# Moving the chunk inverses' traffic in DRAM from SP's queue to ScalarE's and GpSimd's queues in a two-layer hybrid backbone

## Chip, cores and metric

The kernel runs on one core of one Trainium2 chip. The metric is the device time of one execution in microseconds (us). The kernel before has a median of 2059.9 us over three runs (2052.24, 2059.9 and 2060.2 us).

## What is computed

A diffusion backbone of two layers over 512 latent tokens and 256 context tokens of width 1024, all in fp32. Each layer has a mixing sub-layer and a squared-ReLU MLP, with RMSNorm, adaLN shift and scale ahead of each and an adaLN gate behind it. Layer 0 mixes by a bidirectional RWKV-7 recurrence (8 heads of 64) beside windowed attention, layer 1 by neighbourhood and global attention. The change is in the recurrence, whose state is updated token by token:

```python
def step(state, inp):
    r_t, w_t, k_t, v_t, kk_t, a_t = inp
    sa = jnp.einsum('bhvk,bhk->bhv', state, -kk_t)
    state = (state * w_t[:, :, None, :] + sa[..., None] * (kk_t * a_t)[:, :, None, :]
             + v_t[..., None] * k_t[:, :, None, :])
    return state, jnp.einsum('bhvk,bhk->bhv', state, r_t)
```

The adaLN vectors are products of the conditioning with w_ada, 6144 columns per layer.

## The kernel before

The recurrence is computed in chunks of 64 tokens, 12 chunks for the 768 tokens, for four pairs of heads (p = 0 to 3) and two directions d. Inside a chunk the update is a unit triangular system of 64 x 64. `prep(p, ...)` makes what the chunks of a pair need, in these stages:

- The front: loads of k and r from a DRAM scratch (849, 850), the heads' norm, the low-rank decays (865) and scans along the tokens (877, 879).
- The factors AR and BK on VectorE (903, 908), then the products of line 917 on TensorE and their masking into the tile XI (918).
- Per pair, four transfers write the two 32 x 32 diagonal blocks of each system from XI to the DRAM scratch nscr (925, 96 KB each in runs of 128 bytes), and one fetches them back as N (928, 384 KB), so that one system stands on each of 96 partitions.
- GpSimd sets X to the identity (930, 931) and makes two products (940, 947); VectorE makes BK's and AR's other halves (942, 945).
- The inverse: 31 steps of two VectorE instructions (954, 955). It ends with a transposed copy into N (958).
- X goes to the scratch xscr and N to tscr (959, 960); four transfers fetch the inverted blocks into XI (966) and two into xw (967).
- The merge: the off-diagonal block from products of 32 x 32 on TensorE (974, 982), in two halves q, with a ScalarE copy behind each product (xw behind 974, XI behind 982).

`chunks(p, ...)` uses XI: transposes (1023, 1029, 1040) of which one takes a value block vr that GpSimd (1038) and ScalarE copy, masked products AK (1052, 1053) and BT (1059, 1060), solving (1068, 1077), outputs (1089 to 1102), the passage from chunk to chunk (1015), and a step per chunk (1131, 1138). What prep makes in its second stage has two buffers, so that pair p+2 waits there for pair p's chunks.

The work is interleaved by generators: while pair p's chunks run, pair p+1's inverse, pair p-1's output and pair p+2's front are advanced, then pair p+2's second stage and pair p+1's merge. A third stream, `ada`, runs beside all of it as filler for TensorE: it loads w_ada in tiles w_raw of 512 KB through SP (341) into three buffers, multiplies each by the conditioning (353; one tile is four products in the program, eight in the profile), and finishes a group of four with a copy adar and a small product (362) and an addition into mod (364). The column products before that (430) stream their own weights through SP (238).

Within these bounds a scheduler of the language sets each engine's order, from its own estimates. Each engine runs its own instructions in order, and an engine that issues a transfer waits in its queue for what the transfer needs.

Of the kernel before, what the change touches and what calls it, by code (L numbers as in the profile page):

```python
# [174 lines left out]
def trunk(ctx: ExitStack, tc: tile.TileContext, xT, cT, vec_d, wada, we, wo_in, wout, wf1, wf2, lw2_d, la2_d, lg2_d,  # L175
          rpb_d, con_d, nm_d, rot_d, out):
    nc = tc.nc
    V, S, G, PE = nc.vector, nc.scalar, nc.gpsimd, nc.tensor
# [212 lines left out]
    nscr = dp.tile([4, 96, 32, 32], F32, name="nscr")  # L391
    xscr = dp.tile([4, 96, 32, 32], F32, name="xscr")
    tscr = dp.tile([4, 96, 32, 32], F32, name="tscr")
# [30 lines left out]
    def product(w, uh, ul, a, b, step=8):  # L424

        hi, lo = w
        ps = one()
        pairs = three(lambda k: hi[:, k, :], lambda k: lo[:, k, :], lambda k: uh[k][:, a:b], lambda k: ul[k][:, a:b], KT)
        for j, (x, y) in enumerate(pairs):
            PE.matmul(ps[:, 0:b - a], x, y, start=j == 0, stop=j == len(pairs) - 1)  # L430
            if j % step == step - 1 and j < len(pairs) - 1:
                yield
        return ps
# [409 lines left out]
    def prep(p, R, rt, iv, sts, res):  # L843
# [47 lines left out]
        xv = XI.rearrange("p c h t -> p (c h) t")  # L891
# [29 lines left out]
        for d in range(2):  # L921
            for b in range(2):
                o = d * 64 + b * 32
                i0 = d * 48 + b * 24
                nc.sync.dma_start(nscr[p, i0:i0 + 24].rearrange("i s t -> s i t"), xv[o:o + 32, :, 32 * b:32 * b + 32])

        N = iv.tile([128, 32, 32], F32, name="N")
        nc.sync.dma_start(N[0:96], nscr[p])
        X = iv.tile([128, 32, 32], F32, name="X")
        G.memset(X[0:96], 0.0)  # L930
        G.memset(X[0:96].rearrange("p a b -> p (a b)")[:, 0::33], 1.0)
# [18 lines left out]
        for s in range(31):  # L950
            a, b = s + 1, 31 - s
# [4 lines left out]
            if s % 2:  # L956
                yield QUIET if s > QS else None
        V.tensor_copy(N[0:96].rearrange("p s i -> p i s"), X[0:96])
        nc.sync.dma_start(xscr[p], X[0:96])
        nc.sync.dma_start(tscr[p], N[0:96])  # L960
        w1 = rt.tile([128, T], F32, name="xw")
        for d in range(2):
            for b in range(2):
                o = d * 64 + b * 32
                i0 = d * 48 + b * 24
# [311 lines left out]
    def front(p):  # L1277

        if p < 4:
            preps[p] = prep(p, R, rt, iv, sts, res)  # L1280
            yield from until(preps[p], FRONT)
# [188 lines left out]
    with ExitStack() as p2:  # L1470
# [17 lines left out]
        for p in range(4):  # L1488
# [42 lines left out]
            t = None  # L1531
# [215 lines left out]
    with ExitStack() as p3:  # L1747
# [13 lines left out]
        with pool("po", 1) as pp:  # L1761
            ws = [W.take() for _ in range(4)]
            po = [pp.tile([128, T], F32, name=f"po{m}") for m in range(6)]
            for ms, gs in ((range(4), GROUPS[:2]), ((4, 5), GROUPS[:2]), ((0, 1), GROUPS[2:])):
                for c, tok in gs:
                    while c == 1 and pend:
                        tick()
                    for m in ms:
                        if m == len(ws):
                            ws.append(W.take())  # L1770
                        p = product(ws[m], *u1, tok.start, tok.stop, 12)
# [119 lines left out]
```

## Time and profile before

| | |
|---|---|
| median of three runs | 2059.9 us |
| profiled execution | 2055.19 us |
| its span, and mean granted clock of TensorE | 2053.4 us, 0.971 |
| TensorE / VectorE / ScalarE / GpSimd busy | 94 / 55 / 40 / 6 % of the span |
| transfers issued by SP and ScalarE | 96544 and 15296 packets |

The span of the profiled execution is 1.8 us shorter than its own time, and that time is 4.7 us below the median. TensorE works at 94% of the span, and its idle time is what other engines and transfers can add. The column products run until some 346 us, the chunks of the four pairs from there until some 701 us, and the MLP and layer 1 after that. Rows of the profile give the start or the length in us, the engine (PE is TensorE, DVE VectorE, ACT ScalarE, POOL GpSimd, SP SyncE, and a q behind it the engine's queue), the line, and the tiles out<-in.

### The profile page before, as it was taken

The page shows a single profiled execution, that of the slowest core. Times are in us where ns is not written, and L with a number is a line of the kernel's source. Part 1 is how long each engine was busy: PE and PEld are TensorE (multiplying, and loading weights), DVE is VectorE, ACT ScalarE, POOL GpSimd, SP SyncE. Part 2 cuts the span into 40 slices and gives each one's busy share as a digit, 9 for nine tenths or more (in the row PEclk, how much of TensorE's full clock was granted, in tenths as well). Part 3 has the DMA queues.
Part 4 walks back from the last instruction along what each step waited for, and adds up shares of the span by engine and source line. Part 5 has one row for each costly group of instructions (what it writes and reads, how often), then busy time and mean ns, then how long its engine had stood idle before and what let it go on. Part 6 is the DMA issues. An engine that isn't in the chain of part 4 may idle for free.

```text
span 2053.4 us, 38620 instructions
## 1 busy us (share of the span) xinstructions
PE 1932.7 (94%) x16412; PEld 1633.5 (80%) x16412; DVE 1124.7 (55%) x1999; ACT 817.0 (40%) x1531; POOL 122.2 (6%) x149
## 2 busy tenths in 40 slices
PE   6999988988888899999999999899999899999997
PEld 3878767666666897888888889898888798888887
DVE  6576477547464377233433345856575575444445
ACT  3466442534335244311322122435686645222332
POOL 1000011011100000000000000001021000000000
PEclk9999989999999999999999999999999999999998
DMA  7422334666634233211221021342111334322221
GB/s 309 149 65 78 108 109 129 209 195 207 207 126 145 71 112 132 73 61 42 83 72 62 32 83 42 103 151 68 51 39 37 123 102 166 102 83 82 97 88 42
DMA packets 112013, 217.47 MB, mean 106 GB/s; under 512 B 38496, under 2 KB 63968, under 8 KB 111328
## 3 DMA queue, kind: packets, MB, share of 16 engines
q1 hardware_dynamic: 96544, 191.66, 28.6%
q10 hardware_dynamic: 15296, 23.33, 3.2%
q8 instruction: 129, 2.11, 0.4%
q14 instruction: 44, 0.36, 0.1%
HBM read 184.29 MB, written 28.05 MB: 103 GB/s over the span
## 4 chain that ended last, share of the span: by engine, by line
PE 63%; DVE 7%; ACT 3%; issue 3%; DMA 2%; POOL 1%; POOLq 0%; ACTq 0%; DVEq 0%; SPq 0%
PE x L1588 45%; PE x L430 5%; PE ax L530 2%; PE ax L511 2%; PE b L1015 1%; PE b L493 1%; PE ad L353 1%; PE b L1077 1%; PE b L494 1%; DMA w_raw<-in_wada_dram 1%; DVE X L955 1%; DVE nacc L288 1%; ACT Z L182 1%; DVE pr L954 1%; POOL r L264 0%
## 5 line engine op out<-in xcount | busy, mean ns | idle before, releaser
L182 ACT ACTIVATE w_hi<-w_raw 128x1024 fp32r<-128x1024 f32 x183 | 192.3, 1058 | 484.1 <-PE x L1588 369.1
L225 DVE TENSOR_TENSOR w_lo<-w_raw,w_hi 128x1024 fp32r<-128x1024 f32 x181 | 220.8, 1223 | 194.6 <-ACT w_hi L182 193.0
L1588 PE MATMUL x<-fl,w_hi 128*128 128x256 f32 (+1 forms) x864 | 290.9, 338 | 3.9 <-DVE fl L1675 3.9
L1588 PE MATMUL x<-uh,w_hi 128*128 128x512 f32 (+1 forms) x864 | 286.7, 337 | 3.0 <-ACT uh L182 3.0
L1588 PE MATMUL x<-fh,w_lo 128*128 128x256 f32 (+1 forms) x864 | 289.4, 336 | 0.0
L1588 PE MATMUL x<-ul,w_hi 128*128 128x512 f32 (+1 forms) x864 | 287.9, 336 | 0.0
L1588 PE MATMUL x<-uh,w_lo 128*128 128x512 f32 (+1 forms) x864 | 287.6, 336 | 0.0
L1588 PE MATMUL x<-fh,w_hi 128*128 128x256 f32 (+1 forms) x864 | 286.9, 337 | 0.0
L1602 DVE TENSOR_TENSOR oa<-x,oa 128x512 f32<-128x512 f32 (+1 forms) x184 | 103.1, 563 | 207.9 <-PE x L1588 207.0
L430 PE MATMUL x<-uh,w_hi 128*128 128x256 f32 (+1 forms) x560 | 190.2, 340 | 1.6 <-ACT po L182 1.3
L430 PE MATMUL x<-uh,w_lo 128*128 128x256 f32 (+1 forms) x560 | 189.1, 338 | 0.0
L430 PE MATMUL x<-ul,w_hi 128*128 128x256 f32 (+1 forms) x560 | 188.5, 337 | 0.0
L1588 PEld LDWEIGHTS x<-fl,w_hi 128*128 128x128 f32 x864 | 164.3, 190 | 22.0 <-DVE fl L1675 4.3
L1588 PEld LDWEIGHTS x<-uh,w_hi 128*128 128x128 f32 x864 | 161.8, 189 | 21.1 <-ACT uh L182 3.9
L1588 PEld LDWEIGHTS x<-fh,w_lo 128*128 128x128 f32 x864 | 164.1, 190 | 17.9
L1588 PEld LDWEIGHTS x<-fh,w_hi 128*128 128x128 f32 x864 | 162.1, 190 | 20.0 <-ACT fh L182 2.5
L1588 PEld LDWEIGHTS x<-ul,w_hi 128*128 128x128 f32 x864 | 162.8, 189 | 17.7
L1588 PEld LDWEIGHTS x<-uh,w_lo 128*128 128x128 f32 x864 | 162.8, 189 | 17.6
L430 PEld LDWEIGHTS x<-uh,w_hi 128*128 128x128 f32 x560 | 107.5, 192 | 12.5 <-issue 2.7
L430 PEld LDWEIGHTS x<-uh,w_lo 128*128 128x128 f32 x560 | 107.7, 192 | 9.4 <-issue 1.2
L430 PEld LDWEIGHTS x<-ul,w_hi 128*128 128x128 f32 x560 | 107.8, 192 | 9.2 <-issue 1.3
L1674 DVE TENSOR_TENSOR rl<-rl 128x512 f32<-128x512 f32 (+1 forms) x108 | 59.3, 550 | 77.7 <-ACT fh L182 77.5
(304 smaller groups left out, 3398.7 us busy)
## 6 DMA issues: line engine op xcount, KB each, us to landing
w_raw<-in_wf_dram SPq DMA_DIRECT2D x128, 512.0 KB
w_raw<-in_wada_dram SPq DMA_DIRECT2D x96, 512.0 KB
w_raw<-in_we_dram SPq DMA_DIRECT2D x21, 512.0 KB
w_raw<-in_wo_in_dram SPq DMA_DIRECT2D x18, 512.0 KB
w_raw<-in_wout_dram SPq DMA_DIRECT2D x16, 512.0 KB
hsc<-h ACTq DMA_DIRECT2D x8, 1024.0 KB
scr<-po ACTq DMA_DIRECT2D x21, 384.0 KB
h<-hsc SPq DMA_DIRECT2D x7, 1024.0 KB
```

Source lines behind the costliest of these rows:

```text
L182: return S.activation(o, i, f, **k)
L225: eng.tensor_tensor(o_lo, x, o_hi.bitcast(F32), op=ALU.subtract)
L288: V.tensor_reduce(acc, sq.rearrange("p k t -> p t k"), axis=AX.X, op=ALU.add)
L353: PE.matmul(ps[o:o + 32, 0:256], si[:, 2 * kp + k, :], w[:, k, j * 256:(j + 1) * 256], start=kp == 0, stop=kp == 3)
L430: PE.matmul(ps[:, 0:b - a], x, y, start=j == 0, stop=j == len(pairs) - 1)
L493: PE.matmul(ps[:, off:off + n], qs, kh, start=True, stop=False)
L494: PE.matmul(ps[:, off:off + n], qs, kl, start=False, stop=True)
L511: PE.transpose(pt[:, (kb - k0) * 128:(kb - k0 + 1) * 128], P[:, kb * 128:(kb + 1) * 128], ident)
L530: PE.matmul(po[h * 64:h * 64 + 64, 0:128], v(h, k), pts[h][:, k], start=k == 0, stop=k == n - 1)
L1588: PE.matmul(o, a, b, start=n == 0, stop=n == len(pairs) - 1)
L1602: tt(oa[:, m, tok], ps, oa[:, m, tok], op=ALU.add)
L1674: tt(r, r, r, op=ALU.mult)
```

## The change

The four writes of the blocks (925) are issued by ScalarE. The fetch of N (928) and the two writes of the result (959, 960) are issued by GpSimd (G). The fetches of the result (966, 967) and all weights stay with SP. Nothing of the data or the arithmetic is changed.

```diff
--- before.py
+++ after.py
@@ -922,10 +922,10 @@
             for b in range(2):
                 o = d * 64 + b * 32
                 i0 = d * 48 + b * 24
-                nc.sync.dma_start(nscr[p, i0:i0 + 24].rearrange("i s t -> s i t"), xv[o:o + 32, :, 32 * b:32 * b + 32])
+                nc.scalar.dma_start(nscr[p, i0:i0 + 24].rearrange("i s t -> s i t"), xv[o:o + 32, :, 32 * b:32 * b + 32])
 
         N = iv.tile([128, 32, 32], F32, name="N")
-        nc.sync.dma_start(N[0:96], nscr[p])
+        G.dma_start(N[0:96], nscr[p])
         X = iv.tile([128, 32, 32], F32, name="X")
         G.memset(X[0:96], 0.0)
         G.memset(X[0:96].rearrange("p a b -> p (a b)")[:, 0::33], 1.0)
@@ -956,8 +956,8 @@
             if s % 2:
                 yield QUIET if s > QS else None
         V.tensor_copy(N[0:96].rearrange("p s i -> p i s"), X[0:96])
-        nc.sync.dma_start(xscr[p], X[0:96])
-        nc.sync.dma_start(tscr[p], N[0:96])
+        G.dma_start(xscr[p], X[0:96])
+        G.dma_start(tscr[p], N[0:96])
         w1 = rt.tile([128, T], F32, name="xw")
         for d in range(2):
             for b in range(2):
```

The scheduler gives all engines another order between the last column products and the end of pair 3's inverse. Three places follow; the numbers behind a tile's name tell its instances apart.

VectorE around the inverse of pair 2, in pair 1's round (b_5034 is the AK product of block 0 of pair 1's chunks), before:

```order
L1053 TENSOR_TENSOR AK<-b_5034,con 128x384
L364 TENSOR_TENSOR mod<-ad,vec 128x8
L377 COPY sh<-mod 128x8 x2
L1060 TENSOR_TENSOR BT<-b_5048,con 128x12x64
L1199 TENSOR_TENSOR t<-b_5111,t 128x768
L942 TENSOR_TENSOR bk_4733<-kds,ei_4063 128x12x64
L948 SCALAR_TENSOR_TENSOR kds<-kds,vec,r 128x768
L364 TENSOR_TENSOR mod<-ad,vec 128x8
L954 TENSOR_TENSOR pr<-X,N 96x31
L955 TENSOR_TENSOR X<-X,pr 96x31
```

and now:

```order
L1201 TENSOR_TENSOR y<-y,r_5170 128x768
L364 TENSOR_TENSOR mod<-ad,vec 128x8
L954 TENSOR_TENSOR pr<-X,N 96x31
L955 TENSOR_TENSOR X<-X,pr 96x31
L954 TENSOR_TENSOR pr<-X,N 96x60
L955 TENSOR_TENSOR X<-X,pr 96x2x30
L954 TENSOR_TENSOR pr<-X,N 96x87
L955 TENSOR_TENSOR X<-X,pr 96x3x29
L954 TENSOR_TENSOR pr<-X,N 96x112
L1053 TENSOR_TENSOR AK<-b_5034,con 128x384
L955 TENSOR_TENSOR X<-X,pr 96x4x28
```

Seven instructions of the inverse stand ahead of AK, and the products 942 and 948 no longer stand between AK and its start. In SP's order, where pair 0's four writes were, there is now the load of r (850), with its wait for VectorE.

Pair 1's merge on ScalarE and on TensorE (b_4879 and b_4906 are the two halves of line 974, b_4937 and b_4964 those of 982). ScalarE before, with what each waits for (DMAHW are the counters of transfers that SP and ScalarE share):

```order
L182 ACTIVATE xw<-b_4879 32x384 [waits DMAHW5_49,DMAHW1_49,PE_49]
L182 ACTIVATE xw<-b_4879 32x384
L182 ACTIVATE xw<-b_4906 32x384 [waits PE_49]
L182 ACTIVATE adar<-ad 128x256 [waits PE_49]
L182 ACTIVATE xw<-b_4906 32x384
L182 ACTIVATE XI<-b_4937 32x12x32 [waits PE_49]
```

and now:

```order
L182 ACTIVATE adar<-ad 128x256 [waits PE_49]
L182 ACTIVATE xw<-b_4879 32x384 [waits PE_49]
L182 ACTIVATE xw<-b_4879 32x384
L925 DMA nscr<-XI 32x24x32 [waits DMAHW5_49,DVE_49]
L925 DMA nscr<-XI 32x24x32 [waits DMAHW0_49]
L925 DMA nscr<-XI 32x24x32 [waits DMAHW2_49]
L925 DMA nscr<-XI 32x24x32 [waits DMAHW5_49]
L182 ACTIVATE xw<-b_4906 32x384 [waits PE_49]
L182 ACTIVATE xw<-b_4906 32x384
```

The four writes of pair 2's blocks stand between the two halves' copies, and the fourth waits on the same counter as the first. TensorE in the same place before:

```order
L974 MATMUL b_4879<-xw,XI 32x32
L353 MATMUL ad<-w_raw,si 32x256 x4
L974 MATMUL b_4879<-xw,XI 32x32 x23
L974 MATMUL b_4906<-xw,XI 32x32 x24
L353 MATMUL ad<-w_raw,si 32x256 x4
L982 MATMUL b_4937<-XI,xw 32x32 x11
L362 MATMUL ad<-con,adar 128x4 x2
L982 MATMUL b_4937<-XI,xw 32x32 x13
L982 MATMUL b_4964<-XI,xw 32x32 x7
L353 MATMUL ad<-w_raw,si 32x256 x4
L982 MATMUL b_4964<-XI,xw 32x32 x17
```

and now:

```order
L974 MATMUL b_4879<-xw,XI 32x32 x22
L362 MATMUL ad<-con,adar 128x4 x2
L974 MATMUL b_4879<-xw,XI 32x32 x2
L974 MATMUL b_4906<-xw,XI 32x32 x17
L353 MATMUL ad<-w_raw,si 32x256 x4
L974 MATMUL b_4906<-xw,XI 32x32 x7
L982 MATMUL b_4937<-XI,xw 32x32 x3
L353 MATMUL ad<-w_raw,si 32x256 x4
L982 MATMUL b_4937<-XI,xw 32x32 x21
L353 MATMUL ad<-w_raw,si 32x256 x8
L982 MATMUL b_4964<-XI,xw 32x32 x24
L362 MATMUL ad<-con,adar 128x4 x2
```

Four tiles (x4, x4, x8) stand between the first products of 974's second half and 982's second half, where one stood before.

TensorE among the column products, some 270 us into the span, the difference:

```order
 L430 MATMUL x_2865<-ul_119,w_hi 128x256
 L430 MATMUL x_2865<-uh_111,w_lo 128x256
+L353 MATMUL ad<-w_raw,si 32x256 x16
+L362 MATMUL ad<-con,adar 128x4 x2
 L430 MATMUL x_2942<-uh_104,w_hi 128x512
 L430 MATMUL x_2942<-ul_112,w_hi 128x512
```

Four tiles in one go, with their finish, stand ahead of the columns x_2942; before, three of them stood behind those.

On GpSimd, N stands behind the products of line 947 in pair 0 and ahead of the copies vr of pair p-1's chunks in the later pairs; xscr and tscr stand ahead of the last of those copies.

## Rows read from the trace of the kernel before

**Rows 1.** Two lines of the profile page: the span, and the busy time of each engine with its share of the span.

```profile
span 2053.4 us, 38620 instructions
...
PE 1932.7 (94%) x16412; PEld 1633.5 (80%) x16412; DVE 1124.7 (55%) x1999; ACT 817.0 (40%) x1531; POOL 122.2 (6%) x149
```

**Rows 2.** Table by stretches (start:end in us, length, busy us of each engine with its instructions, granted clock of TensorE as a share of full speed, DMA share, GB/s): the end of the column products, then the four rounds of the chunked mixer.

```profile
269.00:346.00 77.00, 74.47 (x397) 60.33 (x395) 51.56 (x107) 22.55 (x31) 5.24 (x4) 0.89 0.41 123
...
360.00:380.00 20.00, 17.35 (x288) 13.89 (x287) 2.77 (x7) 9.95 (x21) 3.04 (x4) 0.74 0.45 117
380.00:420.00 40.00, 37.21 (x637) 24.19 (x635) 33.01 (x86) 18.40 (x31) 0.37 (x1) 1.00 0.79 263
...
448.00:475.00 27.00, 24.98 (x488) 16.61 (x482) 8.06 (x16) 12.61 (x26) 6.65 (x6) 0.87 0.77 225
475.00:520.00 45.00, 40.20 (x623) 27.75 (x615) 35.66 (x89) 19.36 (x31) 4.19 (x4) 0.92 0.59 200
...
548.00:578.00 30.00, 26.35 (x567) 18.54 (x568) 10.30 (x21) 12.71 (x26) 6.66 (x6) 0.89 0.60 177
578.00:620.00 42.00, 36.89 (x754) 28.47 (x754) 31.28 (x84) 12.46 (x27) 0.69 (x2) 1.00 0.47 137
```

**Rows 3.** What SP's queue waited for between 200 and 700 us: line, releaser, us in total, times, longest.

```profile
SPq L341 <- PE ad L353: 139.0, 51, 14.6
...
SPq L959 <- DVE X L955: 29.3, 3, 17.0
...
SPq L925 <- DVE XI L918: 25.5, 2, 24.3
...
SPq L341 <- DMA w_raw<-in_wada_dram: 22.2, 20, 3.3
```

**Rows 4.** SP's queue in time: pair 0's blocks, pair 1's result, pair 2's blocks, input, result and fetch, pair 3's blocks (start us, us, instruction, count).

```profile
269.31 3.03 SPq L925 DMA_DIRECT2D nscr<-XI  x4
...
414.49 0.34 SPq L959 DMA_DIRECT2D xscr<-X  x1
...
460.33 3.86 SPq L925 DMA_DIRECT2D nscr<-XI  x4
...
466.60 0.34 SPq L928 DMA_DIRECT2D N<-nscr  x1
...
510.06 0.34 SPq L959 DMA_DIRECT2D xscr<-X  x1
...
517.12 0.89 SPq L966 DMA_DIRECT2D XI<-xscr  x2
...
553.38 4.71 SPq L925 DMA_DIRECT2D nscr<-XI  x4
```

**Rows 5.** All issues of line 925 between 240 and 720 us: least/median/longest ns of one.

```profile
L925 SPq DMA_DIRECT2D nscr<-XI x16: 326/645/2067, 269.3 to 556.1; - x16
```

**Rows 6.** VectorE in time, pairs 2 and 3: the last mask of pair 2, the product block 0 of pair 1's chunk waits for, and the first step of the inverse of pairs 2 and 3.

```profile
448.47 0.69 DVE L918 TENSOR_TENSOR XI<-b,con 128x512 f32<-128x512 f32 x1 [0.50 <-PE b L917]
...
461.43 0.56 DVE L1053 TENSOR_TENSOR AK<-b,con 128x384 f32<-128x384 f32 x1 [7.78 <-PE b L1052]
...
474.66 0.18 DVE L954 TENSOR_TENSOR pr<-X,N 96x31 f32<-96x31 f32 x1
...
577.81 0.18 DVE L954 TENSOR_TENSOR pr<-X,N 96x31 f32<-96x31 f32 x1
```

**Rows 7.** Chain of waits that ended last, three pieces of it: start us, us, what.

```profile
441.54 5.57 DMA w_raw<-in_wada_dram
...
542.33 4.47 DMA w_raw<-in_wada_dram
...
583.99 5.76 DMA w_raw<-in_wada_dram
```

**Rows 8.** TensorE: all adaLN products between 345 and 701 us (count, busy us, mean ns, idle before them and its releasers); then pieces of the timeline in pair 1's merge, three of TensorE and two of ScalarE, and the first product of pair 2's merge.

```profile
L353 PE MATMUL ad<-w_raw,si 128*32 128x256 f32 x608 | 52.4, 414 | 7.1 <-DMA w_raw<-in_wada_dram 5.7 <-DVE mod L364 1.5
...
449.08 1.70 PE L974 MATMUL b<-xw,XI 32*32 32x32 f32 x94
450.71 0.64 PE L353 MATMUL ad<-w_raw,si 128*32 128x256 f32 x8
...
452.54 0.82 PE L982 MATMUL b<-XI,xw 32*32 32x32 f32 x40
...
450.06 1.48 ACT L182 ACTIVATE xw<-b 32x384 f32<-32x384 f32 x3 [1.16 <-PE b L974]
...
451.97 0.48 ACT L182 ACTIVATE xw<-b 32x384 f32<-32x384 f32 x1
...
549.93 0.75 PE L974 MATMUL b<-xw,XI 32*32 32x32 f32 x34
```

**Rows 9.** Beside one another: VectorE's product L908 alone and beside GpSimd's L940.

```profile
258.73 0.95 DVE L908 TENSOR_TENSOR bk<-t,ei 128x768 f32<-128x768 f32 x1
...
261.13 2.54 DVE L908 TENSOR_TENSOR bk<-t,ei 128x768 f32<-128x768 f32 x1
...
262.81 2.54 POOL L940 TENSOR_TENSOR t<-ic,k 128x768 f32<-128x768 f32 x1
```

**Rows 10.** GpSimd in time: two copies into a chunk's value block, one of pair 0's chunk and one (two instructions) of pair 1's, and the idle time before them with its releaser.

```profile
407.64 0.37 POOL L1038 COPY vr<-v 128x192 f32<-128x192 f32 x1 [29.30 <-PE b L1040]
...
460.67 0.46 POOL L1038 COPY vr<-v 128x64 f32<-128x64 f32 x2 [8.10 <-PE b L1040]
```

## Prediction

> **What bounds the kernel now.** I read the page first, then a table by stretches, then what SP's queue waited for, and last the timelines of single engines in the rounds that the change touches. The page says that TensorE is busy for 94% of the span and VectorE for 55% [rows 1]. So a transfer or an issue is worth only what it takes out of TensorE's idle time, and the reader should look for where that is. The table by stretches shows it [rows 2]. While the column products still run (269 to 346 us) TensorE idles 77.00 - 74.47 = 2.53 us in 77. In the rounds after that it idles more: 2.65 of 20, 2.79 of 40, 2.02 of 27, 4.80 of 45, 3.65 of 30, 5.11 of 42. All that this change can give lies there, and the three stretches in which the 31 steps of an inverse run on VectorE (380 to 420, 475 to 520, 578 to 620 us) hold 2.79 + 4.80 + 5.11 = 12.70 us of it.
>
> The waits of SP's queue come next, since the change is made there [rows 3]. SP stands 139.0 us for adaLN products of TensorE, because a weight buffer has to come free; that is SP running ahead, and costs nothing. It stands 29.3 us for the inverse's result (line 959) and 25.5 us for the masked blocks (line 925), and whatever is queued behind those waits is late. The price of that lateness is on TensorE's side: the 608 adaLN products between 345 and 701 us idled 5.7 us in all for a weight tile [rows 8]. The chain of waits holds landings of such tiles of 4.47 to 5.76 us [rows 7].
>
> **The change part by part.** *SP's queue freed.* It loses four issues per pair on line 925 (0.645 us median, 16 of them [rows 5]) and three more of 0.34 us [rows 4]. That is 4 x 0.645 + 3 x 0.34 = 3.6 us of SP per pair, on an engine that waits 139 us for TensorE, so it counts nothing. What can count is the idle time of 5.7 us for weight tiles. I take 0 and keep -5.7 as the bound: with three buffers, a tile's load starts when TensorE frees a buffer, and SP then has mostly nothing else before it. In pair 0 SP isn't even freed: where the blocks' issues stood (269.31 us [rows 4]) there is now the load of r, which itself waits for VectorE.
>
> *The inverse starts earlier in VectorE's order.* The new order puts the first seven of pair 2's instructions ahead of the AK product of pair 1's chunk, where before the whole inverse stood behind it. The trace says what that is worth: pair 2's last mask ended at 449.2 us, its blocks left SP only at 460.33, 11 us late, and N could be fetched at 466.60; the inverse began at 474.66, and pair 3's at 577.81 [rows 4, 6]. VectorE was busy for only 8.06 of the 27 us from 448 to 475 and 10.30 of the 30 from 548 to 578, and for 35.66 of the next 45 and 31.28 of 42 [rows 2]. Work moved from the full stretch into the empty one relieves the chunk's products that share VectorE with it. Bounds: 0, and the whole idle time of 12.70 us. I take half, -6.4 us, because part of that idle time is for ScalarE's copies and for weight tiles.
>
> *Four issues on ScalarE in the merge.* The blocks of pair p+1 now stand in ScalarE's queue among the copies xw and XI of pair p's merge, for three of the four pairs. Before, in pair 1's merge, three of the four copies went at 450.06 and the last at 451.97 us, and TensorE's second half of the merge followed closely [rows 8]. Now the four issues hold the copies behind them. Bounds of that hold: four issues at 0.645 us, 2.58 us, and the longest such group on SP, 4.71 us [rows 4, 5], plus a landing. The fourth issue waits on the same counter as the first (DMAHW5 in the order shown), and from the last block's issue (460.33 + 3.86 = 464.19) to the fetch of N (466.60) a landing takes at most 2.41 us [rows 4]; so 4.71 + 2.41 = 7.12 us at most. I take 4.71, pair 3's row, because it already has weight transfers beside it. TensorE has cover: four adaLN tiles of 0.64 us [rows 8] stand between the halves of the merge now, 2.56 us. Uncovered 4.71 - 2.56 = 2.15 us, in three merges +6.5 us; between 0 and 3 x 7.12 = 21.4 us.
>
> *A fourth adaLN tile among the column products.* TensorE now takes four tiles (16 products in the order) in one go. There are three buffers, so the fourth tile's load can be issued only when the first is used up. A landing takes 4.47 us, the two tiles between take 2 x 0.64: 4.47 - 1.28 = +3.2 us, between 0 (loaded in time by a longer lead) and 5.76 us, the longest landing shown [rows 7, 8].
>
> *Three issues on GpSimd.* The trace has no transfer issued from GpSimd. Its nearest row for GpSimd working beside VectorE is line 908: 0.95 us alone, 2.54 us beside a GpSimd product [rows 9]. If each of three transfers in the three later pairs slowed one VectorE instruction so, that is 9 x 1.59 = 14.3 us of VectorE time; only what falls into the inverse and isn't idle anyway reaches TensorE, and one instruction per pair, 3 x 1.59 = 4.8 us, is my upper bound. I take 0, as the fetch has slack: pair 2's result was fetched from 517.12 us on, and the merge that uses it began at 549.93 [rows 4, 8]. The page "GPSIMD Engine Reference" of the Trainium skill (section "1. Specifications") says that GpSimd's port to SBUF is shared with VectorE and that instructions with two SBUF inputs contend; line 908 agrees with it for arithmetic, 2.54 against 0.95 us, and whether writing descriptors does the same no row shows. By that rule all of the steps of an inverse, which have two SBUF inputs, would feel it, and the sum would be higher by up to the 4.8 us. The page "DMA: Bandwidth & Descriptors" (section "Specifications") speaks against the move too: it gives about 1 us to the first byte from GpSimd's queue and about 0.6 us from SP's or ScalarE's; by it each pair's chain of three would be some 1.2 us longer, an estimate from that page, and no row here shows it.
>
> **Sum.** 0 - 6.4 + 6.5 + 3.2 + 0 = +3.3 us. Against the profiled execution's own time, 2055.2 us (its span is 2053.4 [rows 1]), that makes 2058.5. The three timed runs have a median of 2059.9, 4.7 us higher, so on that scale **2063.2 us**. That is within 0.5% (10.3 us), which is about what a measurement of this kernel can tell from no change.
>
> **Rivals.** *A: the early inverse pays in full (faster).* All 12.70 us of idle time go, and the 5.7 us for weight tiles, while the ScalarE issues are covered and only the column stage's 3.2 us and one uncovered merge of 2.15 remain: -18.4 + 5.4 = -13.0, 2046.9 us. For it: VectorE stands nearly empty right before each inverse [rows 2]. Against: the merge can't start before the next round anyway, and the fetch had slack. Chance 0.18.
>
> *B: ScalarE's queue becomes the wait in each merge (slower).* The copies xw and XI feed the second half of the merge, and everything in the next chunk stands behind it on TensorE. If the cover of adaLN tiles fails, because its own fourth tile is late for the reason given above, each merge pays 4.71 us: 14.1 + 3.2, and nothing from the inverse, as what is gained there is lost at the next merge: +17.3, 2077.2 us. It decides when the copy behind the last block issue starts more than 2.56 us after the copy before the first one. For it: four issues in a row with waits on the counters between them. Against: in pairs 2 and 3 the blocks are ready close to the merge's start. Chance 0.22.
>
> *C: GpSimd's queue holds the chunk's copies.* GpSimd now waits for the end of the inverse to store xscr, and the copies vr of line 1038 are queued behind. In pair 0's chunk such a copy ran at 407.64 us and the store was possible only at 414.49 [rows 4, 10]; likewise pair 1's copies at 460.67 stood free and now follow N, which waits for the blocks to land. If the inverse isn't earlier, the copy is 6.9 us late, and the products of that block with it: +3.3 + 6.9 = +10.2, 2070.1 us. The earlier inverse speaks against it. Chance 0.10.
>
> *D: the change doesn't do what it says.* SP, freed of these waits, stands at the next one (r behind VectorE, the fetch behind xscr), all weights arrive as before and ScalarE's issues are hidden: 2059.9 us. Chance 0.05.
>
> **How the numbers follow.** My forecast has 0.45. A and the forecast's lower tail give 0.20 for faster; B, a part of C and the upper tail 0.28 for slower; the rest, 0.52, is within 0.5%. The range reaches from A's 2046 to somewhat beyond B, 2082, since B's hold has an upper end of 7.12 us a merge; the bounds of the other costs lie inside it.
>
> **What would show it.** Right: in pair 1's merge a gap of about 4.7 us between two xw copies, filled by the four issues, and TensorE idle for some 2 us there; pair 2's blocks leaving at about 451 instead of 460.33; its inverse starting near 465 instead of 474.66; a wait for a weight tile of about 3 us before 285 us; SP's waits for L918 and L955 gone from its list; less TensorE idle time in the three inverse stretches, by half. Wrong: the stretches after an inverse no shorter although it began 10 us earlier (the merge wasn't waiting for it); copies of line 1038 that wait for GpSimd's own queue (C); or steps of the inverse visibly longer beside GpSimd's issues.

## The result and the profile after

The changed kernel takes 2080.6 us (median of four runs, 2072.8 to 2082.3) against 2056.6 for the kernel before (four runs, 2052.2 to 2060.2): a ratio of 1.011, interval 1.0073 to 1.0147, so some 24 us slower. The fourth run has moved the median of the kernel before from 2059.9 to 2056.6 us. The forecast was 2063.2 us, 3.3 us over its base and within 0.5%; the measured time lies inside the stated range, near its upper end, and on the side that had a chance of 0.28.

The page of the changed kernel, answering to [rows 1]:

```profile
span 2080.3 us, 38638 instructions
...
PE 1947.6 (94%) x16412; PEld 1642.9 (79%) x16412; DVE 1125.4 (54%) x1999; ACT 816.9 (39%) x1531; POOL 130.8 (6%) x161
```

The span is 26.9 us longer and TensorE is still busy for 94% of it. So the loss is not simply idle time: 14.9 us of it are busy time, for the same 16412 products. Where it arises is seen best from the end of one pair's last mask (918) to the next one's, as every round has nearly the same work there (some adaLN tiles and a part of line 974 lie on another side of a border, so that rounds 1 and 2 compare best by their sum). First the kernel before (stretch, length, busy us of the engines from TensorE on, granted clock, DMA share, GB/s): the column products up to pair 1's mask, the rounds up to the masks of pairs 2 and 3, up to pair 3's merge, and up to the MLP:

```profile
269.30:357.60 88.30, 80.78 (x552) 64.44 (x552) 62.86 (x121) 24.64 (x37) 9.93 (x7) 0.86 0.44 133
357.60:449.20 91.60, 80.86 (x1569) 58.36 (x1563) 54.52 (x126) 38.87 (x73) 6.68 (x9) 0.94 0.65 200
449.20:551.00 101.80, 90.95 (x1656) 64.08 (x1654) 58.90 (x130) 38.76 (x74) 13.01 (x12) 0.92 0.63 202
551.00:622.30 71.30, 62.59 (x1276) 46.81 (x1268) 39.25 (x100) 24.64 (x53) 7.35 (x8) 0.95 0.52 152
622.30:691.40 69.10, 57.98 (x1268) 47.31 (x1263) 33.31 (x44) 34.84 (x60) 4.87 (x5) 0.93 0.31 103
```

and the changed kernel, with the same borders:

```profile
271.60:367.90 96.30, 83.51 (x544) 66.37 (x546) 62.15 (x123) 24.14 (x37) 12.13 (x10) 0.84 0.43 130
367.90:472.10 104.20, 87.04 (x1650) 61.98 (x1641) 55.58 (x126) 40.01 (x75) 8.93 (x12) 0.87 0.62 195
472.10:578.40 106.30, 95.95 (x1575) 66.07 (x1572) 58.84 (x128) 38.13 (x73) 15.33 (x15) 0.84 0.59 181
578.40:649.50 71.10, 63.06 (x1270) 47.68 (x1270) 40.19 (x98) 24.12 (x52) 9.72 (x11) 0.88 0.46 134
649.50:721.30 71.80, 60.24 (x1267) 49.94 (x1263) 33.01 (x44) 34.63 (x60) 3.98 (x5) 0.88 0.30 99
```

The five stretches grow by 8.0, 12.6, 4.5, -0.2 and 2.7 us, together 27.6 (449.7 against 422.1), rounds 1 and 2 by 17.1 (210.5 against 193.4). TensorE's busy time in them goes from 373.2 to 389.8 us (+16.6), its idle time from 48.9 to 59.9 (+11.0). The granted clock falls in each, from 0.86-0.95 to 0.84-0.88. A reader should stop at that column: products at the lower of TensorE's two levels, 1.2 and 2.4 GHz, count as busy, and a table of busy shares alone would hide them.

Which products they are, the table of groups says. All 640 adaLN products from 262 to 740 us before (count | busy us, mean ns | idle just before them, and its releasers), answering to the first row of [rows 8]:

```profile
L353 PE MATMUL ad<-w_raw,si 128*32 128x256 f32 x640 | 54.5, 412 | 7.1 <-DMA w_raw<-in_wada_dram 5.7 <-DVE mod L364 1.5
```

and after:

```profile
L353 PE MATMUL ad<-w_raw,si 128*32 128x256 f32 x640 | 67.5, 457 | 18.5 <-DMA w_raw<-in_wada_dram 14.7 <-DVE mod L364 3.7
```

13.0 us more busy and 11.4 us more idle time in front of them: a sum of 24.4 us, against the 26.9 that the span is longer, stands at this one line, the filler. It waits 14.7 us for weight tiles instead of 5.7. That is where the time shows, and not yet what causes it (e14 below).

SP's queue, answering to [rows 3] (line, releaser, us in total, times, longest):

```profile
SPq L966 <- DMA xscr<-X: 29.1, 4, 17.6
...
SPq L850 <- DVE kds L948: 21.1, 1, 21.1
```

The waits for 918 and 955 are gone. SP now waits 29.1 us for xscr to land (9.5 before), in place of the 29.3 for the inverse's end, and 21.1 us for VectorE's product 948, ahead of r. So SP is not much freer: these waits take 50.2 us instead of 64.3 (with the 25.5 of 918). What changed is the order of what it sends.

**The column products.** SP's load of k and TensorE's norm of it (405) before:

```profile
272.50 0.45 SPq L849 DMA_DIRECT2D k<-scr  x1
...
282.66 1.50 PE L405 MATMUL x<-con,t 128*128 128x2 f32 x12 [0.17 <-ACT t L182]
```

and now, SP in pair 0's place, then TensorE:

```profile
278.56 8.93 SPq L341 DMA_DIRECT2D w_raw<-in_wada_dram  x4
287.60 0.37 SPq L849 DMA_DIRECT2D k<-scr  x1
...
286.03 1.08 PE L353 MATMUL ad<-w_raw,si 128*32 128x256 f32 x8 [6.66 <-DMA w_raw<-in_wada_dram]
...
294.61 1.40 PE L405 MATMUL x<-con,t 128*128 128x2 f32 x12
```

The load of k, which before left SP right behind pair 0's blocks, stands behind four weight tiles and leaves at 287.60. The fourth adaLN tile on TensorE waits 6.66 us for its weights, and the norm of k follows at 294.61.

**Pair 0's merge.** ScalarE, then TensorE:

```profile
367.94 0.37 ACTq L925 DMA_DIRECT2D nscr<-XI  x1
369.90 0.84 ACT L182 ACTIVATE gl<-gl 128x768 f32<-128x768 f32 x1 [9.52 <-DVE go L380]
369.92 7.03 ACTq L925 DMA_DIRECT2D nscr<-XI  x3
377.06 0.38 ACT L182 ACTIVATE adar<-ad 128x256 f32<-128x256 f32 x1 [6.32 <-DMA nscr<-XI]
...
368.69 1.71 PE L974 MATMUL b<-xw,XI 32*32 32x32 f32 x96
373.66 0.64 PE L353 MATMUL ad<-w_raw,si 128*32 128x256 f32 x8 [3.26 <-DMA w_raw<-in_wada_dram]
377.49 1.01 PE L362 MATMUL ad<-con,adar 128*128 128x4 f32 x4 [3.20 <-ACT adar L182]
378.84 2.79 PE L353 MATMUL ad<-w_raw,si 128*32 128x256 f32 x24 [0.33 <-DVE mod L364]
381.55 2.23 PE L982 MATMUL b<-XI,xw 32*32 32x32 f32 x74
```

Behind the first issue stands gl, and behind it three issues that take 7.03 us; only then come adar and the copies xw. TensorE ends 974 at 370.4, waits 3.26 us for a weight tile and 3.20 for adar, works through three more tiles at 0.93 us each, and begins 982 at 381.55: 11.2 us between. Before, 982 followed 974 after 0.8:

```profile
359.83 0.24 PE L982 MATMUL b<-XI,xw 32*32 32x32 f32 x2 [0.79 <-ACT xw L182]
```

The chain of waits shows what became of the blocks:

```profile
367.94 8.68 DMA nscr<-XI
...
376.65 5.03 DMA nscr<-XI
...
382.20 6.95 DMA N<-nscr
```

The first block needs 8.68 us to land, the fourth, which waits on the first one's counter, 5.03 more, N 6.95. Before, all four had landed at most 6.1 us after the first issue (nscr issued at 357.63, N at 363.71).

**Pair 2**, answering to [rows 6] and to the forecast's marks (last mask and first step of the inverse on VectorE, the first two issues on ScalarE):

```profile
471.37 0.69 DVE L918 TENSOR_TENSOR XI<-b,con 128x512 f32<-128x512 f32 x1 [0.24 <-PE b L917]
...
489.17 0.19 DVE L954 TENSOR_TENSOR pr<-X,N 96x31 f32<-96x31 f32 x1 [4.46 <-DMA N<-nscr]
...
472.96 0.89 ACTq L925 DMA_DIRECT2D nscr<-XI  x2
```

The first issue follows the mask within 0.9 us instead of 11, and the inverse starts 17.1 us after it instead of 25.5. That part came as forecast, and bought nothing (e7 below).

### The profile page after: what moved, and what is told of

The parts are those of the page before. It is cut to its first block, busy times and chain, and to the rows that moved or that the text cites. A ratio compares the mean times of both kernels' runs of the same rounds, so it can differ in the third digit from the quotient of the medians.

```text
span 2080.3 us, 38638 instructions
## 1 busy us (share of the span) xinstructions
PE 1947.6 (94%) x16412; PEld 1642.9 (79%) x16412; DVE 1125.4 (54%) x1999; ACT 816.9 (39%) x1531; POOL 130.8 (6%) x161
## 4 chain that ended last, share of the span: by engine, by line
PE 76%; DVE 9%; issue 5%; DMA 5%; ACT 4%; POOL 1%; SPq 0%; POOLq 0%; ACTq 0%; DVEq 0%
PE x L1588 45%; PE x L430 11%; PE ax L530 3%; PE ax L511 2%; PE b L493 2%; DMA nscr<-XI 1%; PE ad L353 1%; PE b L494 1%; DMA w_raw<-in_wada_dram 1%; PE b L1015 1%; PE b L1077 1%; DMA N<-nscr 1%; PE b L865 1%; POOL r L264 1%; DVE pr L954 1%
```

## Experiments

All ratios are against the kernel before, on the same chip. The change itself has 1.011 (1.0073 to 1.0147) and 24.0 us.

| kernel | ratio, interval | us over before |
|---|---|---|
| e1: only the blocks on ScalarE | 1.0121 (1.0094 to 1.0147) | 26.3 |
| e2: only N, xscr, tscr on GpSimd | 1.0023 (1.0004 to 1.0041) | 5.4 |
| e4: only xscr, tscr on GpSimd | 0.9996 (0.998 to 1.0013) | -0.6 |
| e5: the change, N left to SP | 1.0066 (1.0043 to 1.0089) | 15.3 |
| e7: the change, AK ahead of the inverse | 1.0135 (1.0105 to 1.0166) | 26.7 |
| e12: the change, merges first | 1.018 (1.0146 to 1.0213) | 38.7 |
| e12b: before, merges first | 0.9996 (0.9983 to 1.0009) | -1.8 |
| e11: two of four writes on ScalarE | 1.0041 (1.0027 to 1.0056) | 7.4 |
| e14: the change, fourth tile behind the columns | 1.0128 (1.0108 to 1.0148) | 28.3 |
| e15: the change, merge's copies on VectorE | 1.0166 (1.0136 to 1.0196) | 35.9 |
| e10: the change, blocks on GpSimd too | 1.0063 (1.0045 to 1.0081) | 12.8 |
| e16: the change, three weight tiles used over and over | 0.9918 (0.9898 to 0.9937) | -15.2 |

### Which part: e1, e2, e4, e5

```diff
e1:  nc.scalar.dma_start(nscr...)   N, xscr, tscr: nc.sync
e2:  nc.sync.dma_start(nscr...)     N, xscr, tscr: G
e4:  nc.sync.dma_start(nscr..., N)  xscr, tscr: G
e5:  nc.scalar.dma_start(nscr...)   N: nc.sync   xscr, tscr: G
```

> Only the four writes of the blocks (925) go to ScalarE; N, xscr and tscr stay with SP. Theory A (ScalarE's issues and the order that they bring cost the time: four adaLN tiles in one go among the column products, 6.7 us of wait in the changed kernel, and the copies xw of pair 0's merge held behind the issues, some 11 us): most of the loss stays, 14 to 20 us over the kernel before. Theory B (the transfers that GpSimd issues are slow, N needs 6.7 to 7.8 us to land, and the inverse waits 26.8 us for it): within 5 us of the kernel before. Under both the inverse waits less for N than 26.8 us.

> Only N, xscr and tscr go to GpSimd; the four writes of the blocks stay with SP, and VectorE's order is nearly that of before, with no step of an inverse ahead of the AK product of block 0. Theory A: within 5 us of the kernel before, since an inverse that starts late anyway doesn't wait for N. Theory B: 12 to 24 us slower, as N lands some 3 to 4 us later in each of the four pairs and xscr, tscr as well.

> Only the result (xscr, tscr) goes to GpSimd; the rest stays with SP. Theory A: within 5 us of the kernel before, perhaps some us faster, since SP no longer stands 29.3 us for the end of the inverses and the fetch has 18 us and more of slack in pairs 0 to 2. Theory B: 3 to 8 us slower, by later landings ahead of pair 3's merge, which has no slack.

> The change with N left to SP: blocks from ScalarE, result from GpSimd. The order is that of the changed kernel, with the inverse ahead of AK. Theory A: near the first of these four kernels; against the changed kernel it gains only what N lands earlier in three rounds, 3 x 3 = 9 us at most, so 10 to 20 us over the kernel before. Theory B: N was the cost, so within 5 us of the kernel before.

The blocks on ScalarE alone cost as much as the whole change (26.3 us, more than the 14 to 20 expected). The result on GpSimd costs nothing, N some 5 us. Theory B fell. In e1 and e5, with the blocks on ScalarE, the scheduler's order is nearly that of the change (four tiles among the columns, steps of the inverse ahead of AK); in e2 and e4 it is nearly that of before. TensorE's wait for weight tiles in e1 is almost that of the change:

```profile
PE ad L353 <- DMA w_raw<-in_wada_dram: 13.9, 8, 4.8
```

e5 is 11 us better than e1, though it only adds the result on GpSimd, and 9 us better than the change, whose interval overlaps with its own; the first was not expected, and its cause stays open.

### ScalarE's hold or VectorE's wait: e7, e12, e12b, e11

```diff
e7   in prep, around the first L954:
+            with tc.issue_after(res["ak"].ins) if not s and "ak" in res else nullcontext():
     (and the round's generators start one step later, so that AK exists)
e12  the change, e12b the kernel before:
-        for t in until(preps[1], READY): ...
         for t in preps[0]: ...
+        for t in until(preps[1], READY): ...
     (and the same swap in rest())
e11
-  nc.scalar.dma_start(nscr...)
+  (nc.scalar if d else nc.sync).dma_start(nscr...)
```

> The change, and the first step of each inverse of pairs 1 to 3 may only stand behind the AK product of block 0 of the round's chunks on VectorE; ScalarE's issues stay inside the merges. Theory A1 (ScalarE's issues hold the merge's copies; by the profile of the changed kernel the merge of pair 0 is 10.8 us longer, the column products 6 to 9 us, and the rounds after it together only some 5.5 us): the loss stays above 14 us over the kernel before, at most 6 us better than the change. Theory A2 (VectorE's wait for N ahead of AK, 10.4 + 4.5 + 7.4 us in pairs 1 to 3, is the loss): within 8 us of the kernel before.

> The change, with the merge of each pair put ahead of the next pair's second stage in the program, so that the copies xw and XI stand ahead of the four issues on ScalarE; AK then also stands ahead of the inverse. Four adaLN tiles stay in one go among the column products. A1: pair 0's merge takes some 5 us instead of 17, and what is left is the column products' 7 us and N's late landing: 5 to 11 us over the kernel before. A2 expects the same total, but with the merge's length unchanged and the gain in the rounds; the first run beside this one tells the two apart. A third theory (A3: the adaLN tiles alone, six more us of waiting for weights, at any place): still 14 us and more over the kernel before.

> The kernel before, with the merge ahead of the next pair's second stage: the control for the run before this one, since that order may cost or gain by itself. A1 and A2 expect within 6 us of the kernel before; if the order itself is worth 6 us or more, the gain of the run before this one is not ScalarE's queue.

> The change, with the two writes of the blocks of direction 0 left to SP and two on ScalarE: the column products have the order of before again (three adaLN tiles). A1: two issues still stand among the copies of pair 0's merge behind the load of gl, so that merge is 5 to 10 us longer than before, and the column products lose nothing: 6 to 14 us over the kernel before. If the hold grows with the number of issues alone, half: about 5 us in that merge.

e7 took VectorE's wait for N nearly away. In the change:

```profile
DVE pr L954 <- DMA N<-nscr: 26.8, 4, 10.4
```

and in e7, where 954 has become line 955:

```profile
DVE pr L955 <- DMA N<-nscr: 5.2, 2, 3.8
```

The time stayed (26.7 us over). So the inverse ahead of AK is not the loss, A2 fell, and taking most of the 26.8 us of VectorE's waiting away gained nothing. e12 has xw and XI ahead of the issues and is the slowest of all, 38.7 us over; the order alone costs nothing (e12b). The hold only moved to the next copy that TensorE needs:

```profile
ACT adar L182 <- DMA nscr<-XI: 13.8, 2, 8.9
```

So my A1, too, had the wrong place: it isn't the merge's copies alone. e11 has no four tiles in one go, and TensorE's wait for weights is that of before; it costs 7.4 us, as A1 expected. So those 7.4 us are not TensorE's wait for weight tiles, and their cause isn't shown:

```profile
PE ad L353 <- DMA w_raw<-in_wada_dram: 5.5, 6, 1.6
```

### The tiles, the copies, the queue: e14, e15, e10

```diff
e14  in ada, around the products of the first group's fourth tile:
+                with tc.issue_after(lastcol[0].ins) if hold and (l, q, kp) == (*which[0], 3) else nullcontext():
e15  xw, XI and adar:
-            act(...)
+            V.tensor_copy(...)
e10
-  nc.scalar.dma_start(nscr...)
+  G.dma_start(nscr...)
```

> The change, with the fourth adaLN tile's products allowed on TensorE only behind the last column product; the merges' order on ScalarE stays. Theory C (four tiles in one go cost the column stage 8 us, of which 6.7 us are the wait for the fourth tile): the column stage back to 88 to 90 us from 96.3, and the whole 14 to 20 us over the kernel before instead of 24. If the tile was only a place where time was lost that something else loses next (the same weights are waited for later): still 22 us and more.

> The change, with the merge's copies xw and XI and the copy adar of the adaLN rows done by VectorE, so that nothing that TensorE waits for in a merge stands behind the four issues on ScalarE. Four tiles stay in the column stage. Theory A1 (ScalarE's queue, held by the issues and their counters, is what costs the rounds): round 1 (mask to mask) back from 104 to 92 to 96 us, and the whole 8 to 14 us over the kernel before, nearly all in the column stage. Theory A4 (the blocks land in 5 to 9 us instead of 3 beside the weights that SP now sends, and TensorE idles for that): round 1 still above 100 us, the whole 18 us and more over.

> The change, with the four writes of the blocks on GpSimd as well: SP is as free as in the change, ScalarE issues nothing of it. A1: within 8 us of the kernel before, less than the change by 16 us or more. A4: still 15 us and more over the kernel before, as the blocks land beside the same weights, and GpSimd's transfers land late (6.7 to 7.8 us).

e14 removed the wait for the fourth tile, and gained nothing. Its SP, ScalarE and TensorE show why:

```profile
276.63 1.28 SPq L341 DMA_DIRECT2D w_raw<-in_wada_dram  x3
278.01 1.15 SPq L852 DMA_DIRECT2D k<-scr  x1
...
288.47 0.93 ACT L182 ACTIVATE t<-k,vec 128x768 f32<-128x768 f32 x1 [11.01 <-DMA k<-scr]
...
289.46 2.72 PE L406 MATMUL x<-con,t 128*128 128x2 f32 x12 [9.56 <-ACT t L182]
```

k is issued behind three weight tiles at 278.01 and ScalarE's first use of it starts at 288.47; TensorE then stands 9.56 us at line 405. The tile's wait had only covered that of k. From pair 0's last mask to the norm of k (405) it is 13.4 us before, 23.0 in the change, 19.8 in e14 and 10.0 in e10, and the column stage lasts 88.3, 96.3, 92.9 and 81.8 us: the later k, the longer the stage (e10 also has less adaLN work there, 2.1 us in place of 4.6 before and 7.4 in the change). Rounds 1 and 2 take 211.3 us in e14, as in the change.

TensorE's wait for weight tiles is another matter. In e14 (353 has become 354) it is nearly that of before, and yet the whole loss stays:

```profile
PE ad L354 <- DMA w_raw<-in_wada_dram: 6.7, 8, 1.6
```

So the length of that wait does not measure the loss. e15 took all of the merge's copies from ScalarE; round 1 still lasts 102.1 us, rounds 1 and 2 together 208.9 against the change's 210.5, and the wait for weights grew (stretch, then releaser, us, times, longest):

```profile
365.90:468.00 102.10, 87.75 (x1606) 62.47 (x1600) 61.51 (x140) 32.24 (x58) 8.73 (x12) 0.85 0.60 188
...
PE ad L353 <- DMA w_raw<-in_wada_dram: 19.2, 11, 6.0
```

That is 35.9 us over the kernel before where A1 wanted 8 to 14: A1's forecast failed. But VectorE is busy for 13.8 us more in rounds 1 and 2 there, so that e15 can hide a gain on ScalarE. e10, with ScalarE free of the blocks, lies at 12.8 us, between what A1 and A4 said, and a loss of that size needs no issue on ScalarE. Its order is another one, and its loss stands in another place: the column stage is 6.5 us shorter than before, round 1 takes 111.4 us. SP's queue, then GpSimd:

```profile
346.69 33.34 SPq L341 DMA_DIRECT2D w_raw<-in_wada_dram  x14
...
385.34 0.34 POOL L1038 COPY vr<-v 128x192 f32<-128x192 f32 x1 [25.00 <-DMA v<-scr]
```

The load of v leaves SP behind these 14 weight tiles, at 380.08, GpSimd's copy waits 25.00 us for it, and TensorE has nothing but adaLN tiles from 366.55 until it multiplies that copy at 385.74. It is k's case once more, with another load.

### The weights: e16

```diff
-            if todo:
+            if todo and len(kept) == 3:
+                todo.pop(0); kept.append(kept.pop(0)); got.append(kept[-1])
+            elif todo:
```

> The change, with the adaLN stream of this stretch using the first three weight tiles again and again: 77 loads of 512 KB shrink to 3, all products, copies and orders of the stream stay (the adaLN vectors come out wrong). ScalarE's issues still stand among the merge's copies and seven and five steps of an inverse still stand ahead of AK, as in the change. Theory W (the order places adaLN tiles in bursts ahead of critical products, TensorE waits there for their weights, 14.7 us against 5.7, works on at a lower clock, and the blocks land late beside the weights): the loss goes, at most 5 us over the kernel before, possibly under it. Theory Q (ScalarE's and VectorE's queues held by the issues, their counters and N): 15 us and more over the kernel before, with those waits as long as in the change. Since the kernel before would also gain its 5.7 us of waiting for weights, anything between 5 and 15 us over is shared.

Some 40 us faster than the change and 15.2 faster than the kernel before, on the side of theory W, which allowed 5 us over it at most. ScalarE and TensorE in pair 0's merge (lines are six higher: 931 is 925, 980 is 974, 988 is 982):

```profile
358.44 0.33 ACTq L931 DMA_DIRECT2D nscr<-XI  x1
...
358.89 2.17 ACTq L931 DMA_DIRECT2D nscr<-XI  x3
...
359.06 1.71 PE L980 MATMUL b<-xw,XI 32*32 32x32 f32 x96
...
363.96 0.95 PE L988 MATMUL b<-XI,xw 32*32 32x32 f32 x48
```

Order and issues are nearly the same (one adaLN tile less stands between 974 and 982), but the three issues take 2.17 us instead of 7.03, and 974 to 982 takes 4.9 us from start to start instead of 12.9. VectorE still waits long for N:

```profile
DVE pr L960 <- DMA N<-nscr: 18.4, 4, 6.7
```

and yet the column stage and rounds 1 and 2 are below those of before, at a clock of 0.94 to 0.96:

```profile
271.20:358.40 87.20, 77.68 (x556) 62.50 (x557) 61.83 (x123) 25.24 (x38) 12.14 (x10) 0.94 0.37 110
358.40:448.30 89.90, 78.28 (x1648) 57.50 (x1640) 54.07 (x126) 38.72 (x74) 8.78 (x12) 0.96 0.16 35
448.30:542.80 94.50, 83.93 (x1596) 58.51 (x1596) 59.69 (x131) 37.85 (x74) 14.99 (x15) 0.96 0.18 46
```

So the loss needs the weights' stream: that much of theory W stands. Theory Q fell for VectorE, whose wait is still 18.4 us long while the loss is gone. For ScalarE it did not fall: its hold shrank together with the weights, so that e16 leaves open whether the hold alone costs time. Nor is it separated how much of the loss is TensorE's wait in front of the filler, how much the loads that stand behind weights, and how much the weights' share of the DMA engines (0.62 in round 1 of the change, 0.16 here). The kernel before without its weights was not run, so that the change's cost in a kernel with no such stream stays open; the 15.2 us can't be credited to the change.

No version with all its weights beats both kernels; e12b's -1.8 us has 1 inside its interval.

## Why the prediction was right in its range and wrong in its steps

The time is inside the range, but not by the sum: that has +3.3 us, and the measured difference is 24. The range reached to 2082 only by the upper end of B's hold, which the runs don't bear out, so that being right was luck.

- **SP's queue freed (taken as 0, bound -5.7): the step that failed.** The bound had the wrong sign. SP sends weights where the blocks stood, and behind them stand the loads that the path needs: k left SP 16.0 us after pair 0's last mask instead of 3.2, and the column stage lost 8.0 us. The wait for weight tiles rose by 9.0 us to 14.7 instead of falling to 0, since the scheduler's order put the filler ahead of its weights; with the lower clock this made 24.4 us at line 353. That the tiles' wait itself is the price is not shown (e14); that the loss needs the weights' stream is (e16), and for the 17.1 us of rounds 1 and 2 the way from the one to the other stays open. I had read SP's 139.0 us of waiting for TensorE as time that "costs nothing" and had not asked what SP would send instead.
- **The inverse earlier (-6.4): failed.** It did start earlier (17.1 us after the mask), and rounds 1 and 2 grew by 17.1 us together. e7 shows that its place on VectorE gains nothing when it is put back. Rival A, which let it pay in full, failed with it.
- **ScalarE's issues (+6.5): not borne out as the price.** In pair 1's merge the gap between the copies is 2.9 us, less than the 4.71 taken; in pair 0's the three issues took 7.03 us, close to the bound of 7.12. But in e15 and e12 taking the copies out of their way gave nothing back, and by e16 the hold is short without the weights' traffic. e11, with two issues, costs 7.4 us for a reason that isn't shown.
- **The fourth tile (+3.2): under-sized.** The wait was 6.66 us, over its bound of 5.76, and the stage lost 8.0. By e14 the tile's wait covers that of k, which stands behind the weights.
- **GpSimd (0): right for the result** (e4, 0.9996), wrong by 5 us for N (e2). N landed in 6.7 to 7.8 us beside the weights, and in a median of 3.8 without the adaLN tiles (e16; its longest, 7.7, too).
- **Rival B** gave 2077.2, near the measured time, but by the hold of the merge's copies, which e15 and e12 speak against. What the trace shows of it is the clause that the filler's own tile would be late (6.66 and 3.26 us). C did not show: TensorE's list of waits has none for a copy of 1038. The first half of D came true, SP stands at r behind VectorE and at the fetch behind xscr; its second half did not, as the order of the weights changed.

The Trainium skill, in "DMA: Bandwidth & Descriptors" (section "Issuing engines are not separate DMA queues"), says that all engines' transfers run interleaved on the same 16 DMA engines, and that issuing from several saves only the time of issue. The runs agree that the transfers of several queues share the engines: the first block needed 8.68 us to land beside the weights, and with the weights gone the same issues passed in 2.17 instead of 7.03 us.

## What to carry to other kernels

Ask of a queue that is relieved what it will send instead, and what urgent load will then stand behind that or land beside it; the bound of such a step is not one-sided. A filler stream is free only while its data is there: where a scheduler orders by its own estimate of transfers, a change of queue can put filler ahead of its data on an in-order engine, and an urgent load behind the filler's data. Look for the loss in busy time too, line by line, and don't believe in a long wait on an engine until taking it away moves the time: here the wait for N, the merge's copies and the filler's wait each went without moving it.

## Not expected of the hardware

A fetch of 384 KB issued by GpSimd landed in 6.7 to 7.8 us beside the weights' stream, and in 3.6 at the least without the adaLN tiles. A 96 KB write in runs of 128 bytes needed 8.68 us beside that stream in one merge and 3.46 in the next. And 16.6 of the 27.6 us lost showed as busy time, at a granted clock of 0.84 to 0.88 instead of 0.86 to 0.95.
